# Second norm of a transformer block by halves of the tokens, and half the token subtractions on GpSimd

## The chip, the cores and the metric

The kernel runs on one core of a Trainium2 chip. The metric is device time in microseconds (us) of one execution. Five engines run their own instruction queues in order and meet only at semaphores: TensorE (PE, with its weight loads shown apart as PEld), VectorE (DVE), ScalarE (ACT), GpSimd (POOL) and SyncE (SP, which only starts DMAs).

## The reference

A block with adaptive norms (a scale, a shift and a gate for each sub-layer) over 512 tokens of width 2048. The last part of it concerns us:

```python
x = x + gt1 * merge_groups(...)             # ends in einsum('btm,md->btd', y, w_out)
h2 = rmsnorm(x, g_norm2) * (1 + sc2) + sh2
x = x + gt2 * conv_ffn(h2, rows, GRID_W, w_up, conv_w, conv_b, w_down)
```

`rmsnorm(x, g)` is `x * rsqrt(mean(x*x) + 1e-6) * g`, with the mean over the 2048 channels of a token. `conv_ffn` multiplies h2 with the gate half and the value half of `w_up`, puts the gate through a 3x3 depthwise convolution and SiLU, multiplies by the value, and projects back with `w_down`. The norm therefore stands between two dense products: no product of `w_up` can start before some token's sum over all channels is known, and that needs the last output columns of `w_out`.

## The kernel before

**Layout.** Activations lie transposed: channel on the partition, token on the free axis. The residual stream is 16 tiles `x2[k]` of 128 channels x 512 tokens. Each fp32 product is made of three products of fp32r parts: `split(hi, lo, x)` casts x to a rounded part `hi` on ACT and subtracts it on DVE (`lo`), and `mm3` accumulates hi·hi, hi·lo and lo·hi. So every weight tile costs ACT a cast (`hi_...`) and DVE a subtraction (`lo_...`) before PE can use it.

**Units.** A unit is 512 output channels as four accumulators (three for the first gate unit) in PSUM banks, over eight weight tiles kp = 0..7 of two contraction steps each. `unit_steps` loads a weight tile, splits it, and issues 6 products per accumulator and tile, each 512 tokens wide. The output projection is units `wo0` to `wo3`. The gate unit `ug0` and the value unit `uv0` follow in the same form; from `ug1` on, the units use Strassen-like sums (`seven`) with 256-wide products.

**The norm.** After each `wo` unit `residual` adds gate times accumulator to `x2[k]` on DVE, `square` squares it on ACT and adds it into a running sum `sqsq` on DVE. After `wo3` the generator `token_rstd` makes, with one-column products, the mean of each token in a 128x4 tile (`ps_rms`), takes 1/sqrt with `mean_rsqrt` (Ln and Exp on ACT, four small DVE operations as a Newton step), and spreads it over the partitions again with products against the identity (`rb_rms`). Eleven products that nothing uses (`idle_products`) stand among these. Then for each k DVE multiplies `x2[k]` with scale and rstd, ACT adds the shift and rounds (`bqh`, the high part of h2), and DVE makes the low part (`bql`). The first gate tile is read in an order that needs only the high parts first (`late`).

**Token sums.** For `seven`, the kernel makes sums and differences of token halves from h2 (`token_sums(j)`, j = 7 down to 0): per j two shifts on ACT, four 128x256 subtractions on DVE, and two splits (`bth`, `btl`). They run beside `ug0` and `uv0`. The convolution of the first gate unit (`cv`, `pads`) starts in the same stretch.

**Order.** A scheduler places the instructions on each engine by dependence and priority; `tc.high_priority()` raises what stands in it, `tc.issue_after(ins)` (wrapped by `behind(queue)`) holds an instruction back behind another, and while `pinned` is set the PE instructions keep the order of the program. Pools with few buffers set when a tile can be written: `whi` and `wlo`, the split weights of `wo`, have two buffers each.

Of the kernel before, what the change touches and what calls it, by code (L numbers as in the profile page):

```python
# [11 lines left out]
F32 = mybir.dt.float32  # L12
# [58 lines left out]
def block_kernel(ctx: ExitStack, tc: tile.TileContext, a: dict, out: bass.AP):  # L71
# [3 lines left out]
    def pool(stack, name, bufs=1, space=None, waits="pool"):  # L75
        if space is None:
            return stack.enter_context(tc.tile_pool(name=name, bufs=bufs, reuse_waits=waits))
        return stack.enter_context(tc.tile_pool(name=name, bufs=bufs, space=space, reuse_waits=waits))

    def sub(o, x, y):  # L80
        V.tensor_tensor(out=o, in0=x, in1=y, op=ALU.subtract)
# [15 lines left out]
    def mm(*args, **kw):  # L97
        ins = PE.matmul(*args, **kw)  # L98
        if pinned[0]:
            tc.keep_in_program_order(ins)  # L100
# [42 lines left out]
    def acc(name, shape=(P, T)):  # L143
        return (banks8[0] if banks8 else psA).tile(list(shape), F32, name=name, tag="acc")
# [44 lines left out]
    def load_split(src, name, n=2, w=512):  # L189
        raw = load_raw(src, name, n, w)  # L190
        with tc.high_priority():
            parts = split_new(raw, name, (n, w))
        fill()
        return parts

    def behind(queue):

        stack = ExitStack()
        for ins in queue:
            stack.enter_context(tc.issue_after(ins))  # L200
        return stack
# [10 lines left out]
            sums = split_new(s, f"b{name}", (4, HW))  # L212
        return plain, sums

    def unit_steps(src, name, xh, xl, accs, late=False, rates=None):

        n = len(accs)
        for kp in range(KP):
            if rates:
                rate[0] = rates[kp]  # L220
            wh, wl = load_split(src[kp], f"{name}_{kp}", w=P * n)
            if kp == 0 and late:

                for m, (ws, xs) in enumerate(((wh, xh), (wl, xh), (wh, xl))):
                    for k in range(2):
                        for i in range(n):
                            mm(accs[i], ws[:, k, P * i : P * i + P], xs[k], start=(m == 0 and k == 0), stop=False)
                continue
            for i in reversed(range(n)) if late and kp == KP - 1 else range(n):
                for kk in range(2):  # L230
                    k = 2 * kp + kk
                    mm3(accs[i], wh[:, kk, P * i : P * i + P], wl[:, kk, P * i : P * i + P],
                        xh[k], xl[k], k == 0, k == KT - 1)
# [783 lines left out]

    st_3 = ExitStack()
    gp = pool(st_3, "gp", 2)
    rp = pool(st_3, "rp")  # L1020
    mod_raw.append(pool(st_3, "mraw3", 4, waits="tile"))
    rate[0] = 2.2
    for g in range(4):
# [21 lines left out]
    def square(k, sums, pl, tag, sl=slice(0, T)):  # L1045

        n = sl.stop - sl.start
        first = not sums
        sq = pl.tile([P, n], F32, name=f"sq{tag}{k}", tag=f"{tag}s" if first else f"{tag}{k}" if k >= KT - 2 else tag)
        S.activation(sq, x2[k][:, sl], AF.Square)  # L1050
# [29 lines left out]
    x2d = [dram.tile([P, T], F32, name=f"x2d{k}", tag=f"x{k}") for k in range(KT)]  # L1080
    sums2 = []
    for n in range(4):
        pinned[0] = n == 3
        accs = unit(a["w_out"][n], f"wo{n}", yh, yl)
        for k in range(4 * n, 4 * n + 4):
            x2.append(ytile(k, f"x2_{k}"))
            nc.sync.dma_start(x2[k], a["xT"][k])
        with tc.high_priority():
            for i in range(4):
                residual(4 * n + i, accs[i], modc[2])  # L1090
                nc.gpsimd.dma_start(x2d[4 * n + i], x2[4 * n + i])
                square(4 * n + i, sums2, rp, "sq")
    with tc.high_priority():
        _, r2 = token_rstd(sums2, rp, "rms2", idle=4)
        idle_products(acc("idle", (P, P)), sums2[0][:, 0:P], 7)
    pinned[0] = False
    assert not fillers
    st_3.close()
    st_h.close()
# [6 lines left out]
    fp = pool(ctx, "fp", waits="tile")  # L1106
    stp = pool(ctx, "stp", 3, waits="tile")
# [4 lines left out]
    def flat(x):  # L1112
        return x.rearrange("p a b -> p (a b)")

    bq = [[operand(j, part, "q", f"bq{part}{j}", (P, 4, HW)) for j in range(KP)] for part in "hl"]
    bt = [[operand(j, part, "t", f"bt{part}{j}", (P, 3, HW)) for j in range(KP)] for part in "hl"]
    h2 = [[flat(b[k // 2][:, 2 * (k % 2) : 2 * (k % 2) + 2, :]) for k in range(KT)] for b in bq]
    with tc.high_priority():
        for k in range(KT):
            sk, bk = modc[4][:, k : k + 1], modc[3][:, k : k + 1]  # L1120
            V.scalar_tensor_tensor(out=x2[k], in0=x2[k], scalar=sk, in1=r2, op0=ALU.mult, op1=ALU.mult)
            S.activation(h2[0][k], x2[k], AF.Identity, bias=bk)
            V.scalar_tensor_tensor(out=h2[1][k], in0=x2[k], scalar=bk, in1=h2[0][k].bitcast(F32), op0=ALU.add,
                                   op1=ALU.subtract)
# [63 lines left out]

    def up_gate(q):
        if q == 0:  # L1190
            accs = unit(a["w_up3"][0], "ug0", *h2, n=3, late=True)
            with tc.high_priority():
                for i, ps in enumerate(accs):
                    S.copy(pads[:, i, 1 : ROWS + 1, 1 : GW + 1], ps.rearrange("p (r c) -> p r c", c=GW))
# [76 lines left out]
    up_gate(0)  # L1271
    st_p.close()
    banks8.append(pool(ctx, "psM", 8, PSUM, waits="tile"))
    for j in reversed(range(KP)):
        token_sums(j)
# [28 lines left out]
    halves = [slice(0, T // 2), slice(T // 2, T)]  # L1304

    class Late:
        at = {}
# [135 lines left out]
```

## Time and profile before

| | |
|---|---|
| median of 3 runs | 2513.3 us (2512.97 to 2513.51) |
| the profiled execution | 2511.87 us, span 2510.1 us |
| mean granted TensorE clock | 0.998 |
| PE busy | 2469.3 us (98%) |
| DVE busy | 1815.0 us (72%) |
| ACT busy | 1024.0 us (41%) |
| POOL busy | 182.5 us (7%) |

The span runs from the first to the last instruction, and the execution's own time is 1.8 us longer. The profiled execution is one of its own: 1.4 us under the median of the three timed ones. PE is busy nearly throughout, so what counts is where PE still waits and what is put into its queue. The norm lies at 1140 to 1149 us of the span, `ug0` follows until 1181.5 and `uv0` until 1214.

### The profile page before, as it was taken

Reading aid. Unit: us, or ns where it says so; the run is one execution under the profiler, and the core shown is the slowest. Engines: PE = TensorE matmul, PEld = TensorE weight load, DVE = VectorE, ACT = ScalarE, POOL = GpSimd, SP = SyncE. Lnnn points to the kernel's source line nnn. Section 1 sums busy time; section 2 is a strip of 40 time slices with the busy share of each in tenths; the row PEclk is TensorE's granted clock in tenths of the full one; section 3 lists DMA queues with packets and bytes.
Section 4 is the critical chain, followed back from the end, with each engine's and each line's share of the span. In section 5 each row is a group of like instructions: output and inputs, shape, how many; then the busy total and the mean of one; then the engine's idle time right before and its main releaser. Section 6 shows DMA issues by size and latency. Waiting matters only on the chain.

```text
span 2510.1 us, 39398 instructions
## 1 busy us (share of the span) xinstructions
PE 2469.3 (98%) x15740; PEld 2204.1 (88%) x15740; DVE 1815.0 (72%) x2880; ACT 1024.0 (41%) x1517; POOL 182.5 (7%) x242
## 2 busy tenths in 40 slices
PE   6999999999999999999999999999999999999998
PEld 4887889888987888888989999999999999999997
DVE  6666754554445877858988787878787878787886
ACT  4224543332213233226454444444444444444445
POOL 0000000000000000000020101010101010101022
PEclk9999999999999999999999999999999999999999
DMA  9741011123334878842373737373636363646464
GB/s 385 271 172 42 26 43 51 51 76 125 110 117 155 286 274 304 299 158 99 108 176 101 168 104 166 107 168 104 167 104 166 107 162 108 161 113 160 113 186 135
DMA packets 121552, 372.20 MB, mean 148 GB/s; under 512 B 13908, under 2 KB 18328, under 8 KB 121368
## 3 DMA queue, kind: packets, MB, share of 16 engines
q1 hardware_dynamic: 94680, 318.29, 37.7%
q0 software_dynamic: 25600, 50.34, 11.4%
q8 instruction: 123, 2.02, 0.3%
q10 hardware_dynamic: 1088, 1.05, 0.1%
q14 instruction: 61, 0.50, 0.1%
HBM read 319.30 MB, written 50.33 MB: 147 GB/s over the span
## 4 chain that ended last, share of the span: by engine, by line
PE 85%; issue 9%; DVE 2%; DMA 2%; POOL 1%; ACT 1%; SPq 0%; DVEq 0%; POOLq 0%; ACTq 0%
PE a L98 19%; PE dn L98 17%; PE uv L98 15%; PE ug L98 14%; PE ga L98 7%; PE po L98 4%; PE wo L98 3%; PE sl L98 1%; PE ps_m L98 1%; DMA raw_m<-in_w_mod 1%; PE cst L98 1%; PE s L98 1%; DMA xl<-in_xT 0%; POOL x2d L1269 0%; DMA x2d<-st 0%
## 5 line engine op out<-in xcount | busy, mean ns | idle before, releaser
L98 PE MATMUL dn<-gh,lo_d 128*128 128x512 f32 x672 | 262.3, 390 | 0.3 <-DVE lo_d L93 0.3
L98 PE MATMUL dn<-gh,hi_d 128*128 128x512 f32 x672 | 261.6, 389 | 0.0
L98 PE MATMUL dn<-gl,hi_d 128*128 128x512 f32 x672 | 261.6, 389 | 0.0
L1215 DVE SCALAR_TENSOR_TENSOR cv<-pads,cwt,cv 128x512 f32<-128x512 f32 x344 | 239.5, 748 | 0.6
L1269 POOL DMA_DIRECT2D x2d<-st x160 | 140.1, 928 | 1142.7 <-ACT st L1268 1057.5
L313 DVE SCALAR_TENSOR_TENSOR sum_m<-raw_m,csil,sum_m 128x512 f32<-128x512 f32 x240 | 180.1, 750 | 9.0 <-DMA raw_m<-in_w_mod 3.1
L93 DVE TENSOR_TENSOR lo_buv<-sum_uv,hi_buv 128x1024 fp32r<-128x1024 f32 x80 | 98.0, 1224 | 103.6 <-ACT hi_buv L92 103.6
L98 PEld LDWEIGHTS dn<-gh,lo_d 128*128 128x128 f32 x672 | 126.1, 188 | 28.9 <-DVE lo_d L93 2.6
L98 PE MATMUL a<-hi_h,hTh 128*128 128x256 f32 x512 | 150.4, 294 | 0.5 <-ACT e L406 0.5
L98 PEld LDWEIGHTS dn<-gl,hi_d 128*128 128x128 f32 x672 | 126.2, 188 | 25.9
L98 PEld LDWEIGHTS dn<-gh,hi_d 128*128 128x128 f32 x672 | 126.2, 188 | 25.6
L98 PE MATMUL a<-hi_h,hTl 128*128 128x256 f32 x512 | 144.7, 283 | 0.0
L98 PE MATMUL a<-lo_h,hTh 128*128 128x256 f32 x512 | 144.7, 283 | 0.0
L92 ACT CAST hi_d<-raw_d 128x1024 fp32r<-128x1024 f32 x86 | 88.6, 1030 | 131.9 <-PE ug L98 70.6
L93 DVE TENSOR_TENSOR lo_d<-raw_d,hi_d 128x1024 fp32r<-128x1024 f32 x86 | 102.9, 1196 | 48.1 <-ACT hi_d L92 47.5
L98 PE MATMUL ug<-bth,hi_bug 128*128 128x256 f32 x480 | 136.7, 285 | 0.1
L98 PE MATMUL uv<-bth,lo_buv 128*128 128x256 f32 x480 | 135.9, 283 | 0.8 <-DVE lo_buv L93 0.8
L98 PE MATMUL uv<-bqh,lo_auv 128*128 128x256 f32 x480 | 135.9, 283 | 0.0
L98 PE MATMUL uv<-bth,hi_buv 128*128 128x256 f32 x480 | 135.9, 283 | 0.0
L98 PE MATMUL uv<-bql,hi_auv 128*128 128x256 f32 x480 | 135.8, 283 | 0.0
L98 PE MATMUL ug<-bqh,lo_aug 128*128 128x256 f32 x480 | 135.8, 283 | 0.0
L98 PE MATMUL uv<-btl,hi_buv 128*128 128x256 f32 x480 | 135.8, 283 | 0.0
(379 smaller groups left out, 7347.2 us busy)
## 6 DMA issues: line engine op xcount, KB each, us to landing
raw_m<-in_w_mod SPq DMA_DIRECT2D x192, 512.0 KB, 5.2
raw_d<-in_w_down SPq DMA_DIRECT2D x82, 512.0 KB, 3.4
raw_ug<-in_w_up SPq DMA_DIRECT2D x80, 512.0 KB, 3.5
x2d<-st POOLq DMA_DIRECT2D x160, 256.0 KB, 5.5
raw_uv<-in_w_up SPq DMA_DIRECT2D x80, 512.0 KB, 6.2
raw_h<-in_w_heads SPq DMA_DIRECT2D x64, 512.0 KB, 3.6
raw_ga<-in_w_gates SPq DMA_DIRECT2D x32, 512.0 KB, 4.5
raw_wo<-in_w_out SPq DMA_DIRECT2D x32, 512.0 KB, 4.8
```

The lines of the kernel that those rows point to most:

```text
L92: cast[0] = S.copy(hi, x).ins
L93: return V.tensor_tensor(out=lo, in0=x, in1=hi.bitcast(F32), op=ALU.subtract).ins
L98: ins = PE.matmul(*args, **kw)
L313: V.scalar_tensor_tensor(out=parts[0], in0=x, scalar=ck, in1=parts[0], op0=ALU.mult, op1=ALU.add)
L1215: V.scalar_tensor_tensor(out=t3, in0=src, scalar=w, in1=t3, op0=ALU.mult, op1=ALU.add)
L1269: nc.gpsimd.dma_start(x2d[k], t, accum_op=ALU.add)
```

## The change

- The last unit of the output projection runs kp 0..5 as before; DVE adds these partial sums to the residual. The products of kp 6 and 7 are then made by halves of the tokens: eight groups (two halves, four accumulators) of 12 products 256 wide, each into a bank of its own, with a residual step and a square per group.
- The norm is done per half: two fp32 products of a matrix of ones against the two tiles of squares (`ss2`) give the mean already spread over the partitions, and `mean_rsqrt` works on 128x256. The one-column products, the spreading products and the eleven idle products are gone. Half 0's `ss2` stands on PE after the first group of half 1.
- h2 of k = 0..3 is made by halves, and the first two weight tiles of the gate unit, split early, are used as 72 products 256 wide: half 0 kp 0, `ss2` of half 1, half 0 kp 1, half 1 kp 0 and 1.
- The splits of gate tiles 2 and 3 are held behind half 0's low parts (`split_queue`), and later steps behind one another (`gate_queue`, `lows`, `sums_queue`).
- Two of the four subtractions of each `token_sums(j)` move to GpSimd.
- The clearing of `pads` on GpSimd and the loads of the convolution's weights come after the norm; the four stores of x2[12..15] come after half 1's residual steps.

The diff, cut to its core:

```diff
-            if kp == 0 and late:
...
-                continue
+            with behind(queue if kp < since + 2 else ()):
+                wh, wl = load_split(src[kp], f"{name}_{kp}", w=P * n)
...
+    def last_halves(steps, x, done):
+        for hf, sl in enumerate(halves):
+            for i in range(4):
+                o = acc(f"wo3_{hf}_{i}", (P, T // 2))
+                for kp, (wh, wl) in steps:
+                    for kk in range(2):
+                        k = 2 * kp + kk
+                        mm3(o, wh[:, kk, P * i : P * i + P], wl[:, kk, P * i : P * i + P],
+                            x[0][k][:, sl], x[1][k][:, sl], k == 2 * steps[0][0], k == KT - 1)
+                done(hf, i, o)
...
     with tc.high_priority():
-        _, r2 = token_rstd(sums2, rp, "rms2", idle=4)
-        idle_products(acc("idle", (P, P)), sums2[0][:, 0:P], 7)
-    pinned[0] = False
+        for i in range(4):
+            residual(12 + i, accs[i], modc[2])
+    steps = [(kp, load_split(a["w_out"][3][kp], f"wo3_{kp}")) for kp in (KP - 2, KP - 1)]
...
+    def half_norm(sl):
+        ss = psb(f"ss2_{sl.start}", (P, T // 2))
+        mm(ss, ones, sums2[0][:, sl], start=True, stop=False)
+        mm(ss, ones, last_sq[0], start=False, stop=True)
+        v, t = (rp.tile([P, T // 2], F32, name=f"{n}_{sl.start}", tag=n) for n in ("rv2", "rt2"))
+        with tc.high_priority():
+            mean_rsqrt(ss, D, v, t, r2[:, sl])
+
+    def out_done(hf, i, o):
+        k, sl = 12 + i, halves[hf]
+        with tc.high_priority():
+            residual(k, o, modc[2], sl)
+            sq = rp.tile([P, T // 2], F32, name=f"sqh{hf}_{i}", tag="sqh" if i == 3 else "sq")
+            S.activation(sq, x2[k][:, sl], AF.Square)
+            if i < 3:
+                add(sums2[0][:, sl], sums2[0][:, sl], sq)
+            else:
+                last_sq[0] = sq
+            if hf:
+                nc.gpsimd.dma_start(x2d[k], x2[k])
+        if hf and i == 0:
+            half_norm(halves[0])
...
+        for k in range(4):
+            split_queue = modulated(k, halves[0])
+    gate_queue = []
+    def gate_done(hf, kp):
+        if hf == kp == 0:
+            half_norm(halves[1])
+            with tc.high_priority():
+                for k in range(4):
+                    gate_queue[:] = modulated(k, halves[1])
+    first_halves(gsteps, ug0, h2, gate_done)
...
-        sub(half(k0, 1), half(k0, 1), half(k1, 1))
+        G.tensor_tensor(out=half(k0, 1), in0=half(k0, 1), in1=half(k1, 1), op=ALU.subtract)
         sub(half(k1, 1), half(k1, 1), half(k0, 0))
         split(flat(bt[0][j][:, 0:2, :]), flat(bt[1][j][:, 0:2, :]), x2[k0])
-        sub(rest(j), half(k1, 1), half(k1, 0))
+        G.tensor_tensor(out=rest(j), in0=half(k1, 1), in1=half(k1, 0), op=ALU.subtract)
...
-            accs = unit(a["w_up3"][0], "ug0", *h2, n=3, late=True)
+            accs = ug0
+            for _ in unit_steps(a["w_up3"][0], "ug0", *h2, accs, late=True, since=2, queue=split_queue):
+                pass
```

The first place is the norm on DVE. Before, its queue reads as follows from the last residual step on; `lo_ug0_0` is the low part of the first gate tile, `rs..._rms2` the small norm tiles, `rb_rms2` the spread rstd in PSUM.

```order
L1043 SCALAR_TENSOR_TENSOR x2_15_9433<-wo3_3_9129,mod2_62,x2_15_9433 128x512
L93 TENSOR_TENSOR lo_ug0_0_9620<-raw_ug0_0_9617,hi_ug0_0_9619 128x768
L93 TENSOR_TENSOR lo_ug0_1_9644<-raw_ug0_1_9641,hi_ug0_1_9643 128x768
L159 TENSOR_SCALAR rs1_rms2_9466<-ps_rms2_9453 128x4
L161 SCALAR_TENSOR_TENSOR rs2_rms2_9467<-rs3_rms2_9468 128x4
L84 TENSOR_TENSOR rs2_rms2_9467<-rs2_rms2_9467,rs1_rms2_9466 128x4
L163 SCALAR_TENSOR_TENSOR rs3_rms2_9468<-rs2_rms2_9467,rs3_rms2_9468 128x4
L1121 SCALAR_TENSOR_TENSOR x2_0_8405<-x2_0_8405,mod4_64,rb_rms2_9475 128x512
```

Now the norm of half 1 reads as follows, after half 0's modulation; `rv2`, `rt2` and `cst` (columns of the constants' tile that are no longer needed) are the norm's 256-wide tiles.

```order
L1183 SCALAR_TENSOR_TENSOR x2_3_8411<-x2_3_8411,mod4_64,cst_58 128x256
L1185 SCALAR_TENSOR_TENSOR bql1_9590<-x2_3_8411,mod3_63,bqh1_9582 128x256
L93 TENSOR_TENSOR lo_ug0_2_9775<-raw_ug0_2_9772,hi_ug0_2_9774 128x768
L93 TENSOR_TENSOR lo_ug0_3_9799<-raw_ug0_3_9796,hi_ug0_3_9798 128x768
L159 TENSOR_SCALAR rv2_256_9649<-ss2_256_9646 128x256
L161 SCALAR_TENSOR_TENSOR rt2_256_9650<-cst_58 128x256
L84 TENSOR_TENSOR rt2_256_9650<-rt2_256_9650,rv2_256_9649 128x256
L163 SCALAR_TENSOR_TENSOR cst_58<-rt2_256_9650,cst_58 128x256
L1183 SCALAR_TENSOR_TENSOR x2_0_8405<-x2_0_8405,mod4_64,cst_58 128x256
L1183 SCALAR_TENSOR_TENSOR x2_1_8407<-x2_1_8407,mod4_64,cst_58 128x256
```

The four small operations have become four 256-wide ones for each half, and those of half 1 stand behind the low parts of gate tiles 2 and 3, which before came only after eleven steps of the modulation.

The second place is the norm on ACT. Before, the queue there is this; `sqsq15` is the last square, `bqh` the high parts of h2, `hi_ug0_...` the high parts of gate tiles.

```order
L92 CAST hi_ug0_0_9619<-raw_ug0_0_9617 128x768
L92 CAST hi_ug0_1_9643<-raw_ug0_1_9641 128x768
L1050 ACTIVATE sqsq15_9451<-x2_15_9433 128x512
L158 ACTIVATE rs2_rms2_9467<-ps_rms2_9453,eps_66 128x4
L160 ACTIVATE rs3_rms2_9468<-rs2_rms2_9467 128x4
L1122 ACTIVATE bqh0_9528<-x2_0_8405,mod3_63 128x512
L1122 ACTIVATE bqh0_9528<-x2_1_8407,mod3_63 128x512
L1122 ACTIVATE bqh1_9529<-x2_2_8409,mod3_63 128x512
```

Now it is this, where `sqh1_...` are squares of half 1.

```order
L1148 ACTIVATE sqh1_1_9513<-x2_13_9366 128x256
L1148 ACTIVATE sqh1_2_9531<-x2_14_9368 128x256
L1184 ACTIVATE bqh0_9581<-x2_0_8405,mod3_63 128x256
L1184 ACTIVATE bqh0_9581<-x2_1_8407,mod3_63 128x256
L1148 ACTIVATE sqh1_3_9549<-x2_15_9370 128x256
L1184 ACTIVATE bqh1_9582<-x2_2_8409,mod3_63 128x256
L1184 ACTIVATE bqh1_9582<-x2_3_8411,mod3_63 128x256
L92 CAST hi_ug0_2_9774<-raw_ug0_2_9772 128x768
L92 CAST hi_ug0_3_9798<-raw_ug0_3_9796 128x768
L158 ACTIVATE rt2_256_9650<-ss2_256_9646,eps_66 128x256
L160 ACTIVATE cst_58<-rt2_256_9650 128x256
L1184 ACTIVATE bqh0_9581<-x2_0_8405,mod3_63 128x256
```

Half 1's Ln (`rt2_256`) stands behind the casts of gate tiles 2 and 3, and half 0's first `bqh` stands behind two squares of half 1.

The third place is DVE beside the first value unit, from the low part of its weight tile 5 to that of tile 6. Before, it reads as follows; `cv...` are taps of the convolution, `sum_ug1` and `lo_aug1` belong to the first Strassen-like unit, `bql4` is a low part of the token sums.

```order
L93 TENSOR_TENSOR lo_uv0_5_10023<-raw_uv0_5_10020,hi_uv0_5_10022 128x768
L87 TENSOR_TENSOR sum_ug1_0_10171<-raw_ug1_0_10169 128x512
L93 TENSOR_TENSOR lo_aug1_0_10173<-raw_ug1_0_10169,hi_aug1_0_10172 128x768
L87 TENSOR_TENSOR sum_ug1_0_10171<-sum_ug1_0_10171,raw_ug1_0_10169 128x256
L1215 SCALAR_TENSOR_TENSOR cv0_10114<-pads_9612,cwt_9608,cv0_10114 128x512
L87 TENSOR_TENSOR sum_ug1_0_10171<-sum_ug1_0_10171,raw_ug1_0_10169 128x256
L93 TENSOR_TENSOR bql4_9540<-x2_10_9102,bqh4_9532 128x256
L93 TENSOR_TENSOR lo_uv0_6_10047<-raw_uv0_6_10044,hi_uv0_6_10046 128x768
```

Now the same place reads as follows.

```order
L93 TENSOR_TENSOR lo_uv0_5_10130<-raw_uv0_5_10127,hi_uv0_5_10129 128x768
L87 TENSOR_TENSOR sum_ug1_0_10278<-raw_ug1_0_10276 128x512
L93 TENSOR_TENSOR lo_aug1_0_10280<-raw_ug1_0_10276,hi_aug1_0_10279 128x768
L87 TENSOR_TENSOR sum_ug1_0_10278<-sum_ug1_0_10278,raw_ug1_0_10276 128x256
L1308 SCALAR_TENSOR_TENSOR cv0_10221<-pads_9770,cwt_9766,cv0_10221 128x512
L87 TENSOR_TENSOR sum_ug1_0_10278<-sum_ug1_0_10278,raw_ug1_0_10276 128x256
L93 TENSOR_TENSOR bql4_9593<-x2_10_9102,bqh4_9585 128x256
L1308 SCALAR_TENSOR_TENSOR cv0_10221<-pads_9770,cwt_9766,cv0_10221 128x512
L93 TENSOR_TENSOR lo_uv0_6_10154<-raw_uv0_6_10151,hi_uv0_6_10153 128x768
```

There are two taps where one stood. From the start of the unit to `lo_uv0_6` there are now 12 taps in DVE's queue, and before there were 5; the 16 subtractions that left DVE stand on GpSimd, behind the last store of x2 and the clearing of `pads`.

More of the change, by code (lines that the diff above doesn't have):

```diff
@@ L213, in load_sums, with unit_steps @@
         return plain, sums
-    def unit_steps(src, name, xh, xl, accs, late=False, rates=None):
+    def unit_steps(src, name, xh, xl, accs, late=False, rates=None, since=0, upto=KP, queue=()):
         n = len(accs)
-        for kp in range(KP):
+        for kp in range(since, upto):
             if rates:
                 rate[0] = rates[kp]
-            wh, wl = load_split(src[kp], f"{name}_{kp}", w=P * n)
-            if kp == 0 and late:
[L224 to L227, printed above, removed]
-                continue
+            with behind(queue if kp < since + 2 else ()):
+                wh, wl = load_split(src[kp], f"{name}_{kp}", w=P * n)
             for i in reversed(range(n)) if late and kp == KP - 1 else range(n):
@@ L232, in unit_steps @@
                     mm3(accs[i], wh[:, kk, P * i : P * i + P], wl[:, kk, P * i : P * i + P],
-                        xh[k], xl[k], k == 0, k == KT - 1)
+                        xh[k], xl[k], k == 0, k == 2 * upto - 1, skip_group_check=since > 0)
                 yield 1.36
@@ L1019, in block_kernel @@
     gp = pool(st_3, "gp", 2)
-    rp = pool(st_3, "rp")
+    st_r = ExitStack()
+    rp = st_r.enter_context(tc.tile_pool(name="rp", bufs=1, side="right"))
     mod_raw.append(pool(st_3, "mraw3", 4, waits="tile"))
@@ L1080, in block_kernel @@
     x2d = [dram.tile([P, T], F32, name=f"x2d{k}", tag=f"x{k}") for k in range(KT)]
+    halves = [slice(0, T // 2), slice(T // 2, T)]
     sums2 = []
-    for n in range(4):
-        pinned[0] = n == 3
+    for n in range(3):
         accs = unit(a["w_out"][n], f"wo{n}", yh, yl)
@@ new lines, in first_halves @@
+    def first_halves(steps, accs, x, done):
+        for hf, sl in enumerate(halves):
+            for kp, (wh, wl) in steps:
+                for w, part in ((wh, 0), (wl, 0), (wh, 1)):
+                    for kk in range(2):
+                        for i, o in enumerate(accs):
+                            mm(o[:, sl], w[:, kk, P * i : P * i + P], x[part][2 * kp + kk][:, sl],
+                               start=(hf == kp == kk == part == 0 and w is wh), stop=False, skip_group_check=True)
+                done(hf, kp)
@@ new lines, in block_kernel @@
+    pinned[0] = True
+    accs = [acc(f"wo3_{i}") for i in range(4)]
+    for _ in unit_steps(a["w_out"][3], "wo3", yh, yl, accs, upto=KP - 2):
+        pass
+    for k in range(12, KT):
+        x2.append(ytile(k, f"x2_{k}"))
+        nc.sync.dma_start(x2[k], a["xT"][k])
+    with tc.high_priority():
+        for i in range(4):
+            residual(12 + i, accs[i], modc[2])
+    steps = [(kp, load_split(a["w_out"][3][kp], f"wo3_{kp}")) for kp in (KP - 2, KP - 1)]
+    gsteps = []
+    for kp in range(2):
+        raw = mod_raw[-1].tile([P, 2, 3 * P], F32, name=f"raw_ug0_{kp}", tag="raw")
+        nc.sync.dma_start(raw, a["w_up3"][0][kp])
+        parts = [rp.tile([P, 2, 3 * P], F32R, name=f"{n}_ug0_{kp}", tag=f"{n}{kp}") for n in ("gh", "gl")]
+        split(*parts, raw)
+        gsteps.append((kp, parts))
@@ new lines, in block_kernel @@
+    last_sq = [None]
+    r2 = cc(C_SEG, T)
+    def half_norm(sl):
[19 more added lines that the diff above has]
+            half_norm(halves[0])
@@ L1097, in block_kernel @@
+    last_halves(steps, (yh, yl), out_done)
     assert not fillers
@@ L1105, in block_kernel @@
     bp = pool(ctx, "bp", waits="tile")
-    fp = pool(ctx, "fp", waits="tile")
-    stp = pool(ctx, "stp", 3, waits="tile")
     def operand(j, part, what, name, shape, dtype=F32R):
@@ L1117, in block_kernel, with modulated @@
     h2 = [[flat(b[k // 2][:, 2 * (k % 2) : 2 * (k % 2) + 2, :]) for k in range(KT)] for b in bq]
-    with tc.high_priority():
[L1119 to L1124, printed above, removed]
+    def modulated(k, sl=slice(0, T)):
+        sk, bk = modc[4][:, k : k + 1], modc[3][:, k : k + 1]
+        x, hi, lo = x2[k][:, sl], h2[0][k][:, sl], h2[1][k][:, sl]
+        V.scalar_tensor_tensor(out=x, in0=x, scalar=sk, in1=r2[:, sl], op0=ALU.mult, op1=ALU.mult)
+        hi_ins = S.activation(hi, x, AF.Identity, bias=bk).ins
+        return hi_ins, V.scalar_tensor_tensor(out=lo, in0=x, scalar=bk, in1=hi.bitcast(F32), op0=ALU.add,
+                                              op1=ALU.subtract).ins
+    ug0 = [acc(f"ug0_{i}") for i in range(3)]
+    with tc.high_priority():
+        for k in range(4):
[8 more added lines that the diff above has]
+    first_halves(gsteps, ug0, h2, gate_done)
+    pinned[0] = False
+    with tc.high_priority(), behind(gate_queue):
+        lows = []
+        for k in range(4, KT):
+            with behind(lows[-2:-1]):
+                ins = modulated(k)
+                lows.append(ins[1])
+            if k == 7:
+                sums_queue = ins
+    st_r.close()
+    fp = pool(ctx, "fp", waits="tile")
+    stp = pool(ctx, "stp", 3, waits="tile")
     def half(k, i):
@@ L1190, in up_gate @@
         if q == 0:
-            accs = unit(a["w_up3"][0], "ug0", *h2, n=3, late=True)
+            accs = ug0
+            for _ in unit_steps(a["w_up3"][0], "ug0", *h2, accs, late=True, since=2, queue=split_queue):
+                pass
             with tc.high_priority():
@@ L1273, in block_kernel @@
     banks8.append(pool(ctx, "psM", 8, PSUM, waits="tile"))
-    for j in reversed(range(KP)):
-        token_sums(j)
+    with behind(sums_queue):
+        for j in reversed(range(KP)):
+            token_sums(j)
     vals = []
@@ L1303, in block_kernel @@
         nc.gpsimd.dma_start(x2[k], x2d[k])
-    halves = [slice(0, T // 2), slice(T // 2, T)]
     class Late:
```

## The prediction

> **What bounds the kernel now.** I read the page first: the engines' busy time says who can be the bound.
>
> ```profile
> PE 2469.3 (98%) x15740; PEld 2204.1 (88%) x15740; DVE 1815.0 (72%) x2880; ACT 1024.0 (41%) x1517; POOL 182.5 (7%) x242
> ```
>
> PE works 98% of the span, so a change gains only by taking time out of PE's queue or out of its few waits. Next come the windows around the norm: the last of the output projection, the norm, the gate unit in two pieces, the value unit, and a stretch of 256-wide products. The columns are length, then busy time and count of PE, PEld, DVE, ACT, POOL, then clock.
>
> ```profile
> 1100.00:1140.27 40.27, 40.27 (x192) 32.37 (x190) 10.93 (x13) 8.26 (x11) 1.08 (x2) 1.00 0.22 78
> 1140.27:1148.74 8.47, 8.22 (x55) 7.81 (x55) 4.99 (x11) 3.49 (x8) 1.09 (x2) 0.80 0.49 175
> 1157.00:1181.20 24.20, 24.20 (x108) 20.03 (x107) 24.18 (x44) 21.29 (x34) 0.00 (x0) 1.00 0.31 101
> 1181.20:1213.90 32.70, 32.70 (x146) 27.08 (x145) 32.69 (x65) 20.07 (x35) 0.00 (x0) 1.00 0.42 139
> 1220.00:1240.00 20.00, 20.00 (x169) 20.00 (x168) 20.00 (x31) 9.07 (x12) 0.00 (x0) 1.00 0.30 94
> ```
>
> Two things matter. A 512-wide product comes every 24.20 / 108 = 0.224 us and a 256-wide one every 20.00 / 169 = 0.118 us. And behind the norm PE never waits, but DVE has nothing to spare either: 24.18 of 24.20 and 32.69 of 32.70 us. What delays DVE there may delay PE. The timeline of the norm shows what PE does in its 8.47 us (start, busy, engine, line, operation).
>
> ```profile
> 1140.05 0.39 PE L98 MATMUL wo<-yTh,lo_wo 128*128 128x512 f32 x1
> 1140.64 3.10 PE L98 MATMUL ps_rms<-cst,sqsq 128*128 128x1 f32 x24 [0.21 <-DVE sqsq L87]
> 1143.79 0.27 ACT L158 ACTIVATE rs_rms<-ps_rms,eps 128x4 f32<-128x4 f32 x1 [1.26 <-PE ps_rms L98]
> 1144.08 0.20 ACT L160 ACTIVATE rs_rms<-rs_rms 128x4 f32<-128x4 f32 x1
> 1144.32 0.16 DVE L161 SCALAR_TENSOR_TENSOR rs_rms<-rs_rms 128x4 f32<-128x4 f32 x1
> 1145.46 1.69 PE L98 MATMUL rb_rms<-cst,rs_rms 128*128 128x128 f32 x8
> 1146.98 1.73 PE L98 MATMUL idle<-sqsq,cst 128*128 128x128 f32 x14
> 1147.18 2.72 DVE L1121 SCALAR_TENSOR_TENSOR x<-x,mod,rb_rms 128x512 f32<-128x512 f32 x4 [2.31 <-PE rb_rms L98]
> 1148.74 0.73 PE L98 MATMUL ug<-bqh,hi_ug 128*128 128x512 f32 x2
> ```
>
> From the start of the last product of `wo` to the first of the gate unit pass 8.69 us, where one product would take 0.22. PE counts as busy, but with small or unused products. Seven idle products show as x14: an fp32 product has two records.
>
> **The change part by part.** *Removed:* these 8.69 - 0.22 = **8.47 us**, if halves cover the norm wholly. That is the most the change can bring.
>
> *Halving:* 96 products of 256 for 48 of 512 in `wo`, 72 for 36 in the gate unit: 168 x 0.118 - 84 x 0.224 = **+1.0**. The new sums of squares are four fp32 products 256 wide; the first norm of the kernel has two of them, as four records.
>
> ```profile
> L98 PE MATMUL ss_c<-sq_c,cst 128*128 128x256 f32 x4 | 1.1, 400 | 0.0
> ```
>
> So 1.1 us per half, in PE's queue: **+2.2**. Both of these are certain.
>
> *The last weight tile of the projection.* Its split waits for a buffer that kp 5 frees.
>
> ```profile
> 1128.92 0.39 PE L98 MATMUL wo<-yTh,lo_wo 128*128 128x512 f32 x1
> 1129.12 1.05 ACT L92 CAST hi_wo<-raw_wo 128x1024 fp32r<-128x1024 f32 x1 [4.81 <-PE wo L98]
> 1129.29 0.48 PE L98 MATMUL wo<-yTh,hi_wo 128*128 128x512 f32 x1
> 1130.20 1.23 DVE L93 TENSOR_TENSOR lo_wo<-raw_wo,hi_wo 128x1024 fp32r<-128x1024 f32 x1 [0.57 <-ACT hi_wo L92]
> ```
>
> Before, kp 6 gave PE 24 x 0.224 = 5.4 us of cover from 1129.29. Now the first group needs kp 7 after six half-wide products, 0.7 us, at 1130.0; the low part, third in order, is there at 1130.20 + 1.23 = 1131.43. That is a wait of about **+1.2** (ends 0.9 and 1.4, by how much of the third product's place I count).
>
> *The first gate product.* For the chain of half 0 I need 256-wide durations.
>
> ```profile
> L158 ACT ACTIVATE scr_c<-ss_c,eps 128x256 f32<-128x256 f32 x1 | 0.5, 474 | 2.5 <-PE ss_c L98 2.5
> L160 ACT ACTIVATE rstd<-scr_c 128x256 f32<-128x256 f32 x1 | 0.4, 417 | 0.0
> L163 DVE SCALAR_TENSOR_TENSOR rstd<-scr_c,rstd 128x256 f32<-128x256 f32 x1 | 0.4, 425 | 0.0
> L1043 DVE SCALAR_TENSOR_TENSOR xf<-dl,mod,xf 128x256 f32<-128x256 f32 x8 | 3.7, 481 | 2.5 <-PE dl L98 2.5
> L1050 ACT ACTIVATE sqfq<-xf 128x256 f32<-128x256 f32 x32 | 12.1, 412 | 9.1 <-DVE xf L1043 8.2 <-DVE sqfq L87 0.8
> L93 DVE TENSOR_TENSOR lo_ug<-raw_ug,hi_ug 128x768 fp32r<-128x768 f32 x5 | 4.8, 953 | 0.0
> ```
>
> After half 0's sums: Ln 0.47, Exp 0.42, two Newton steps 0.86, a residual step of half 1 that stands between (0.48), the last Newton step 0.43, `x2_0` 0.48, another residual step 0.48, then on ACT the square behind it 0.41 and `bqh0` 0.41. That is 4.44, and eight handovers of 0.05 (Exp ended at 1144.28, DVE began at 1144.32) make 4.84. PE has three groups, 36 x 0.118 = 4.25. Stall **+0.6**.
>
> *Half 1's norm.* This is the dear place. From the first gate product PE has 36 half products and the second pair of sums, 4.25 + 1.1 = 5.35 us. DVE has in its queue ahead of the next `bqh`: an addition 0.42, three low parts 1.44, `x2_3` 0.48, the wait for its ACT step 0.41, its low part 0.48, then `lo_ug0_2` and `lo_ug0_3` 1.91, the four norm steps 1.71, `x2_0` 0.48, and ACT 0.41: 7.74, with six handovers 8.0. Half 1's first product waits **+2.7**. The ends: 0, if the scheduler's queue were met with DVE far ahead, which nothing in the sum allows, and 3.3 if every handover costs twice this.
>
> So far: -8.47 + 1.0 + 2.2 + 1.2 + 0.6 + 2.7 = **-0.8**: the stall is handed on, not removed.
>
> *The stretch behind it.* DVE loses 16 subtractions and gains 16 half steps for 8 whole ones; GpSimd gets the subtractions.
>
> ```profile
> 1179.83 1.43 DVE L81 TENSOR_TENSOR x<-x,x 128x256 f32<-128x256 f32 x4
> L1215 DVE SCALAR_TENSOR_TENSOR cv<-pads,cwt,cv 128x512 f32<-128x512 f32 x11 | 7.9, 762 | 0.0
> L1347 POOL TENSOR_TENSOR o<-xf,r3s 128x256 f32<-128x256 f32 x10 | 7.2, 748 | 35.8 <-ACT r3s L1338 35.8
> L1194 ACT COPY pads<-ug 128x512 f32<-128x512 f32 x3 | 1.8, 586 | 0.8 <-PE ug L98 0.8
> ```
>
> A subtraction costs DVE (1.43 - 0.42) / 3 = 0.34 us in a row, so 16 x 0.34 = 5.4 are saved; the half steps cost back about 1.0. But seven convolution taps more stand ahead of `lo_uv0_6` in the new order; at 0.66 each (0.76 less the overlap) that is 4.6. DVE is as full as before, and each wait of it goes through. On GpSimd a subtraction takes 0.75. DVE's third step of the last three j each follows a GpSimd step, 3 x (0.75 - 0.34) = 1.2; the casts `bth` behind GpSimd's second step pass on about as much, 1.2; and the copy of the gate's accumulators to `pads`, now behind casts that wait for GpSimd, holds the first value product for one copy, 0.6. Together **+3.0**, between 0 (all of the 5.4 as slack) and 6.5 (16 handovers of 0.41, none hidden).
>
> *Does GpSimd take DVE's time?* Two places of the trace show both at work.
>
> ```profile
> 522.43 0.29 POOL L915 TENSOR_SCALAR_AFFINE_SELECT ed<-ed 128x128 f32<-128x128 f32 x1 [59.33 <-ACT ed L912]
> 525.66 1.46 POOL L915 TENSOR_SCALAR_AFFINE_SELECT ed<-ed 128x128 f32<-128x128 f32 x3 [0.76 <-ACT ed L912]
> 525.26 1.23 DVE L93 TENSOR_TENSOR lo_h<-raw_h,hi_h 128x1024 fp32r<-128x1024 f32 x1 [0.51 <-ACT hi_h L92]
> 768.55 3.64 POOL L915 TENSOR_SCALAR_AFFINE_SELECT ed<-ed 128x128 f32<-128x128 f32 x8 [77.86 <-ACT ed L912]
> 768.15 0.69 DVE L84 TENSOR_TENSOR qs<-qs,qk 128x512 f32<-128x512 f32 x1
> 770.24 0.78 DVE L84 TENSOR_TENSOR qs<-qs,qk 128x512 f32<-128x512 f32 x1
> ```
>
> A GpSimd step of 0.29 alone became three in 1.46 while DVE read two tiles, and DVE's 0.69 became 0.78 beside GpSimd. So they do exclude each other, at least 0.09 per step for a small GpSimd step. For a step of 0.75 the price lies between 0.09 and 0.75; most of the steps here stand on a full DVE, so I take a third of the upper end, 0.25: 16 x 0.25 = **+4.0** (ends 1.4 and 12.0).
>
> The Trainium skill ("SBUF — State Buffer", section "SBUF: two separate sides") says that a DVE operation with two SBUF inputs and a GpSimd operation that reads SBUF hold a shared port pair as an exclusive lock for the whole instruction. The rows above agree as far as they go. By that rule alone, with DVE always the one that waits, the term would be the upper end, 12.0.
>
> The sum: -0.8 + 3.0 + 4.0 = **+6.2**, so 2511.9 + 6.2 = 2518.1 for an execution like the profiled one. The median of the runs stands 1.4 above that one, so I forecast **2519.5**. Differences of under 0.2% (5.0 us) I count as the same, about what a measurement of this kernel can tell from no change: 2508.3 to 2518.3.
>
> **The rivals.** *No contention:* GpSimd and DVE share without loss beyond 0.09 per step, and the last term shrinks to at most 1.4. For it: the second of the two places. Against: the first. -0.8 + 3.0 + 0.7 = +2.9, 2516.2, within 0.2%.
>
> *Everything is covered* (not slower): the low parts of gate tiles 2 and 3 and the norm of half 1 run early enough, and the 5.4 us that DVE saves absorb every wait for GpSimd. What remains is -8.47 + 1.0 + 2.2 + 1.2 = -4.1, 2509.2; without the wait for `lo_wo` -5.3, 2508.0. It decides at the first product of half 1: if DVE's 8.0 us are 5.4, it holds. Against it is the sum of rows above.
>
> *Full lock:* each GpSimd subtraction holds DVE for its 0.75. Waits for GpSimd's results then lie inside that time, so 12.0 takes the place of 4.0 and of the 2.4 of waits: -0.8 + 0.6 + 12.0 = +11.8, 2525.1. For it: the place at 525 us. Against: a DVE step that started first makes GpSimd wait instead.
>
> A smaller one: the clock. In the norm's window the granted clock was 0.80, and PE then lost nothing that counted. After a wait of 2.7 us full-size products could run slower for a while; 8.47 x 0.20 = 1.7 us is what that window lost. It lies inside my range.
>
> **How the numbers follow.** Forecast (+4 to +9) 0.45; no contention 0.25; everything covered 0.15, of which 0.04 below 2508.3; full lock 0.15. Faster is 0.04. The same is the rest of "covered" (0.11), no contention (0.25) and the lowest part of the forecast (0.04): 0.40. Slower 0.56. The range goes from 2509.2 (covered) to 2525.1 (full lock), leaving out about half of each of these two, 0.15. The forecast's own range is 2517 to 2522.5.
>
> **What would show it.** In the new profile: a PE wait of about 1.2 at `lo_wo` of the first half group; a wait under 1 at the first gate product and of 2 to 3 at half 1's, ended by ACT's `bqh`; PE waits for `lo_uv` in the value unit; DVE operations of 256 columns beside GpSimd longer than 0.42. I am wrong if the first product of half 1 follows its predecessor closely, or if the value unit still takes 32.7 us.

## The result

The changed kernel takes 2524.27 us (median of 6 runs, 2520.43 to 2525.23) and the kernel before 2513.14 in the runs beside it: a ratio of 1.0041 with a 95% interval of 1.0028 to 1.0054, or 10.3 us slower (7.0 to 13.6). The profiled execution has a span of 2520.1 us, against 2510.1. The page shows what has grown:

```profile
PE 2470.4 (98%) x15778; PEld 2206.0 (88%) x15778; DVE 1825.0 (72%) x2888; ACT 1027.0 (41%) x1527; POOL 200.5 (8%) x258
```

PE works as long as before, to 1.1 us. DVE, which was to be relieved, works 10 us longer, and POOL 18. So 8.9 of the 10 us are idle time of PE. The timeline of PE has these places (start, busy, operation, in brackets the idle time and what ended it); the rows without a bracket are landmarks, the first product of gate tile 2 and of the first Strassen-like unit.

```profile
1132.44 0.39 PE L98 MATMUL wo<-yTh,lo_wo 128*128 128x256 f32 x1 [0.76 <-DVE lo_wo L93]
1144.58 1.02 PE L98 MATMUL ug<-bqh,gh_ug 128*128 128x256 f32 x6 [0.46 <-ACT bqh L1184]
1152.60 1.02 PE L98 MATMUL ug<-bqh,gh_ug 128*128 128x256 f32 x6 [2.64 <-ACT bqh L1184]
1156.99 0.88 PE L98 MATMUL ug<-bqh,hi_ug 128*128 128x512 f32 x3
1184.23 0.50 PE L98 MATMUL uv<-bqh,hi_uv 128*128 128x512 f32 x1 [1.94 <-ACT pads L1287]
1194.79 0.50 PE L98 MATMUL uv<-bqh,hi_uv 128*128 128x512 f32 x1 [2.06 <-ACT hi_uv L92]
1197.24 0.79 PE L98 MATMUL uv<-bqh,lo_uv 128*128 128x512 f32 x1 [1.72 <-DVE lo_uv L93]
1224.08 0.28 PE L98 MATMUL ug<-bqh,hi_aug 128*128 128x256 f32 x1
```

The landmarks of the kernel before, and where kp 6 of the last `wo` unit begins in the changed one:

```profile
1157.04 0.39 PE L98 MATMUL ug<-bqh,hi_ug 128*128 128x512 f32 x1
1181.52 0.39 PE L98 MATMUL uv<-bqh,hi_uv 128*128 128x512 f32 x1
1214.15 0.28 PE L98 MATMUL ug<-bqh,hi_aug 128*128 128x256 f32 x1
```

```profile
1130.25 0.36 PE L98 MATMUL wo<-yTh,hi_wo 128*128 128x256 f32 x1
```

Counted from kp 6 of the last `wo` unit (1129.29 before, 1130.25 now):

| until the first product of | before | now | difference |
|---|---|---|---|
| gate tile 2 | 27.75 | 26.74 | -1.0 |
| the value unit | 52.23 | 53.98 | +1.75 |
| the Strassen-like unit | 84.86 | 93.83 | +9.0 |

(The remaining 1 us of the span lies ahead of kp 6, where nothing was changed; the first `wo` product differs by as much between the two executions, and by some 2 us between others.) So between these two executions the part up to gate tile 2 is 1.0 us shorter (the clock has a share in that, as e8 shows below), and the stretch behind it, where GpSimd subtracts, costs 10. In the value unit the granted clock falls too, at the second of the two waits and behind it (columns as in the prediction, the clock is the number after POOL):

```profile
1195.00:1200.00 5.00, 3.28 (x9) 2.26 (x9) 5.00 (x9) 2.19 (x6) 2.25 (x2) 0.62 0.24 79
1200.00:1205.00 5.00, 5.00 (x17) 4.00 (x16) 4.93 (x9) 2.79 (x5) 0.00 (x0) 0.70 0.26 82
1205.00:1210.00 5.00, 5.00 (x23) 4.14 (x23) 5.00 (x8) 1.35 (x3) 0.00 (x0) 1.00 0.32 105
```

A product counts as busy for 0.39 us but the next may follow after 0.22, so a wait costs 0.17 more than its idle time. The value unit grew from 32.63 to 39.85 us: 2.23 + 1.89 for the two waits, and the other 3.1 fits the clock, of which the first two rows lack 5 x 0.38 + 5 x 0.30 = 3.4 us, a part of it while PE stood. The groups of DVE and POOL in this stretch show why DVE was late:

```profile
L1185 DVE SCALAR_TENSOR_TENSOR bql<-x,mod,bqh 128x512 fp32r<-128x512 f32 x12 | 9.6, 824 | 0.1
L1183 DVE SCALAR_TENSOR_TENSOR x<-x,mod,cst 128x512 f32<-128x512 f32 x12 | 9.1, 784 | 0.0
L93 DVE TENSOR_TENSOR btl<-x,bth 128x512 fp32r<-128x512 f32 x8 | 6.4, 812 | 0.0
L81 DVE TENSOR_TENSOR x<-x,x 128x256 f32<-128x256 f32 x8 | 5.7, 747 | 2.0 <-POOL x L1230 2.0
L93 DVE TENSOR_TENSOR btl<-x,bth 128x256 fp32r<-128x256 f32 x8 | 4.8, 614 | 0.0
L1233 POOL TENSOR_TENSOR x<-x 128x256 f32<-128x256 f32 x8 | 9.2, 1166 | 6.7 <-DVE btl L93 6.7
L1230 POOL TENSOR_TENSOR x<-x,x 128x256 f32<-128x256 f32 x8 | 8.3, 1046 | 15.0 <-ACT x L1228 12.7 <-DVE x L81 2.4
```

Before, the same five groups took 747, 743, 692, 422 and 425 ns. A 256-wide subtraction of DVE takes 0.75 or 0.61 on average in place of 0.42, and one of GpSimd 1.05 to 1.17 in place of 0.75: each engine holds up the other.

Two of the three new waits are ended by ACT, behind casts that waited for GpSimd or for a late DVE. The clearest is the value unit's wait for `hi_uv`; ACT's rows ahead of it are these:

```profile
1192.10 0.62 ACT L92 CAST bth<-x 128x512 fp32r<-128x512 f32 x1 [2.92 <-POOL x L1230]
1193.91 0.83 ACT L92 CAST hi_uv<-raw_uv 128x768 fp32r<-128x768 f32 x1
```

The cast of `hi_uv` stands behind a cast of the token sums that waited 2.92 us for a subtraction of GpSimd.

### The profile page after: what moved, and what is told of

The parts are those of the page before. It is cut to its first block, busy times and chain, and to the rows that moved or that the text cites. A ratio compares the mean times of both kernels' runs of the same rounds, so it can differ in the third digit from the quotient of the medians.

```text
span 2520.1 us, 39519 instructions
## 1 busy us (share of the span) xinstructions
PE 2470.4 (98%) x15778; PEld 2206.0 (88%) x15778; DVE 1825.0 (72%) x2888; ACT 1027.0 (41%) x1527; POOL 200.5 (8%) x258
## 3 DMA queue, kind: packets, MB, share of 16 engines
q10 hardware_dynamic: 1088, 1.05, 0.1%
## 4 chain that ended last, share of the span: by engine, by line
PE 46%; issue 3%; DVE 2%; DMA 1%; POOL 0%; ACT 0%; DVEq 0%; POOLq 0%; ACTq 0%
PE uv L98 16%; PE dn L98 15%; PE ug L98 14%; DMA raw_uv<-in_w_up 1%; DVE cv L1308 1%; DVE lo_d L93 0%; DMA x2d<-st 0%; PE dl L98 0%; DVE btl L93 0%; DVE o L84 0%; POOL x L1233 0%; ACT hi_d L92 0%; POOL x L1230 0%; PE ps_rmsf L98 0%; DVE o L1437 0%
## 5 line engine op out<-in xcount | busy, mean ns | idle before, releaser
L307 DVE SCALAR_TENSOR_TENSOR sum_m<-raw_m,csil,sum_m 128x512 f32<-128x512 f32 x240 | 180.0, 750 | 10.3 <-DMA raw_m<-in_w_mod 4.3
L98 PE MATMUL ug<-bqh,hi_aug 128*128 128x256 f32 x480 | 135.8, 283 | 0.0
```

The lines of the kernel that those rows point to most:

```text
L307: V.scalar_tensor_tensor(out=parts[0], in0=x, scalar=ck, in1=parts[0], op0=ALU.mult, op1=ALU.add)
```

## The experiments

The theory: GpSimd's subtractions cost the 10 us, mainly because GpSimd and DVE shut each other out of SBUF while DVE is full. Rivals: the reordering around them costs it; only the waits for GpSimd's results cost it; the clock costs it.

**e1, the subtractions back on DVE.**

```diff
-        G.tensor_tensor(out=half(k0, 1), in0=half(k0, 1), in1=half(k1, 1), op=ALU.subtract)
+        sub(half(k0, 1), half(k0, 1), half(k1, 1))
...
-        G.tensor_tensor(out=rest(j), in0=half(k1, 1), in1=half(k1, 0), op=ALU.subtract)
+        sub(rest(j), half(k1, 1), half(k1, 0))
```

> The changed kernel with all 32 token subtractions back on DVE; the norm by halves stays. If GpSimd is what costs the 9.8 us behind the first six gate products, what is left is the norm's own balance of -0.8 us: 1 to 2 us faster than before or the same, no PE wait over 1 us in the value unit, granted clock 1.00 there. Rival: the reordering (splits held back, pads later) costs it: then it stays 6 us or more slower than before, with the waits on pads and on hi_uv still there. The 2.6 us wait of half 1's first gate product should stay in both.

Measured: 1.0001 (0.9992 to 1.0010) of before. The table of PE's waits from 1120 to 1270 us (total, times, longest) has only those of the norm left, and the clock falls behind the long one:

```profile
PE ug L98 <- ACT bqh L1184: 3.1, 2, 2.6
PE wo L98 <- DVE lo_wo L93: 0.8, 1, 0.8
```

```profile
1152.00:1156.00 4.00, 4.00 (x23) 4.00 (x23) 3.36 (x7) 1.72 (x5) 0.00 (x0) 0.59 0.20 67
```

The reordering that stays in e1 is not the cause. (The taps go back with the subtractions: 4 stand ahead of `lo_uv0_6` here, against 12 in the changed kernel.) The norm's 1.0 us is missing here; the clock's lower share takes 4 x 0.41 = 1.6 us. In the changed kernel's own profile it did not fall behind the same wait.

**e2, only the subtractions on GpSimd**, in the kernel before (the diff of e1 turned round).

> The kernel before, with its norm as it was, and only the 16 token subtractions on GpSimd. If GpSimd is the cost, 5 to 10 us slower than before, with PE waits in the value unit for lo_uv or hi_uv that before did not have. Rival (the reordering costs, not GpSimd): within 1 us of before, since DVE gets 5.4 us of work less.

Measured: 1.0028 (1.0016 to 1.0039), 7 us slower. PE's waits:

```profile
PE uv L98 <- DVE lo_uv L93: 3.5, 2, 1.9
PE uv L98 <- ACT hi_uv L92: 2.0, 2, 1.4
```

The kernel before gets new waits for `lo_uv` and `hi_uv` from GpSimd alone (not the one for `pads`), although DVE is handed 5.4 us less work by the prediction's estimate.

**e3, dummy subtractions that nobody waits for.**

```diff
         split(bt[0][j][:, 2, :], bt[1][j][:, 2, :], half(k1, 1))
+        for c in range(2):
+            G.tensor_tensor(out=scr, in0=bt[1][j][:, c, :].bitcast(F32), in1=bt[1][j][:, 2, :].bitcast(F32),
+                            op=ALU.subtract)
```

> The kernel before with 16 extra GpSimd subtractions of the same size beside it, whose result nothing reads (two for each j, behind its last low part); the rest is untouched, the output is that of before. Nobody waits for GpSimd, so only the sharing of SBUF is left. If GpSimd and DVE shut each other out, DVE's 256-wide subtractions beside them take 0.8 to 1.0 us in place of 0.42 and the kernel is 2 to 7 us slower. Rival (only the waits for GpSimd's results cost): DVE's durations stay, and the time is within 0.5 us of before.

Measured: 1.0027 (1.0017 to 1.0038). DVE's order is that of before, row for row. Its timeline has pairs of equal steps, the first of each before 1200 us, the second after it, when GpSimd's steps get through beside them. Below them stand GpSimd's own rows:

```profile
1198.77 0.94 DVE L93 TENSOR_TENSOR lo_uv<-raw_uv,hi_uv 128x768 fp32r<-128x768 f32 x1
1199.63 0.41 DVE L93 TENSOR_TENSOR bql<-x,bqh 128x256 fp32r<-128x256 f32 x1
1203.43 0.97 DVE L93 TENSOR_TENSOR bql<-x,bqh 128x256 fp32r<-128x256 f32 x1
1205.47 1.49 DVE L93 TENSOR_TENSOR lo_uv<-raw_uv,hi_uv 128x768 fp32r<-128x768 f32 x1
```

```profile
1177.28 2.01 POOL L1145 TENSOR_TENSOR scr<-btl 128x256 f32<-128x256 f32 x2 [34.64 <-DVE btl L93]
1180.05 2.22 POOL L1145 TENSOR_TENSOR scr<-btl 128x256 f32<-128x256 f32 x2 [0.76 <-DVE btl L93]
1185.32 27.74 POOL L1145 TENSOR_TENSOR scr<-btl 128x256 f32<-128x256 f32 x12 [3.04 <-DVE btl L93]
```

A GpSimd step that gets through costs a DVE step about half a us whatever its size (0.41 to 0.97, 0.94 to 1.49). Step by step against the trace of before, sixteen DVE steps are longer, as many as there are dummies, by 0.46 to 0.55 us each and 8.2 in all. That alone, with no result waited for, accounts for a loss as large as e2's. The row of 27.74 us shows the other side: the first of its twelve steps lasts 15.34 us, from 1185.32 to 1200.66, and until 1200 DVE's steps all have their normal length.

**e4, useless products against the clock**, in the changed kernel.

```diff
+    idle = acc("idle", (P, HW))
+    pinned[0] = True
-    for _ in unit_steps(a["w_up3"][1], "uv0", *h2, accs):
-        pass
+    for n, _ in enumerate(unit_steps(a["w_up3"][1], "uv0", *h2, accs)):
+        if n == 5:
+            for _ in range(4):
+                mm(idle, ones, cc(C_ID, HW), start=True, stop=True)
+    pinned[0] = False
```

> The changed kernel with four products of constants (fp32, 256 wide, about 2.3 us of PE, result unused) put into PE's queue at the place where it waits 2.1 us for hi_uv in the value unit. If the lower granted clock behind the waits (0.62 and 0.70) costs 3.4 us, useless work makes the kernel 1 to 3 us faster than the changed kernel, 2521 to 2523 us, with a clock near 1.00 there. Rival (the clock follows something else, or costs nothing): the same as the changed kernel or up to 1 us slower.

Measured: 1.0037 (1.0025 to 1.0050), no different from the changed kernel: the gain of 1 to 3 us did not come. PE's waits:

```profile
PE uv L98 <- DVE lo_uv L93: 3.8, 3, 1.8
PE uv L98 <- ACT pads L1287: 1.9, 1, 1.9
PE uv L98 <- ACT hi_uv L92: 0.4, 1, 0.4
```

In the value unit the clock stayed at 1.00, and a new wait of 1.8 us for `lo_uv` came later. DVE looks like the bound there, and slow products filled time in which PE would have waited. The scheduler also put three taps more ahead of that `lo_uv`, so how much of the 3.1 us was free time is not settled.

**e5, useless products in half 1's wait**, on e1. PE is pinned there, so the other engines' order is that of e1.

```diff
                 done(hf, kp)
+            if hf == 0:
+                for _ in range(4):
+                    mm(idle, ones, cc(C_ID, T // 2), start=True, stop=True)
```

> As e1 (halves, all subtractions on DVE), with four products of constants (fp32, 256 wide, result unused) in PE's queue where it waits 2.6 us for the first product of half 1. The order on the other engines is that of e1. In e1's trace the clock fell to 0.59 behind this wait, which cost about 1.5 us. If that is why the halves bring nothing, the wait shrinks to under 1 us, the clock stays at 1.00, and the kernel is 1 to 1.5 us faster than e1, about 1 us faster than before. Rival (the clock falls in any case, or its time was hidden): the same as e1.

Measured: 0.9991 (0.9982 to 1.0000), an interval that still overlaps e1's. The clock stays at 1.00, and the wait is filled (x8 are the four products):

```profile
1148.87 1.89 PE L98 MATMUL idle<-cst 128*128 128x256 f32 x8
1151.67 1.02 PE L98 MATMUL ug<-bqh,gh_ug 128*128 128x256 f32 x6 [0.92 <-ACT bqh L1187]
```

**e6, two accumulators at a time**, on e1.

```diff
-            for i in range(4):
-                o = acc(f"wo3_{hf}_{i}", (P, T // 2))
+            for pair in ((0, 1), (2, 3)) if hf == 0 else ((0,), (1,), (2,), (3,)):
+                outs = {i: acc(f"wo3_{hf}_{i}", (P, T // 2)) for i in pair}
                 for kp, (wh, wl) in steps:
+                    for i in pair:
```

> As e1, but in half 0 the last two weight tiles of the output projection are used for two accumulators at a time (kp 6 for both, then kp 7 for both), so that kp 7 is wanted 0.7 us later. If the 0.76 us wait for lo_wo is paid in full, the kernel is 0.6 to 0.7 us faster than e1 and the wait is under 0.2. Rival: later waits take it back (the first gate product then waits 0.5 us more), no gain.

Measured: 0.9997 (0.9988 to 1.0006). The wait falls by 0.5, not to under 0.2, and the later ones keep their length:

```profile
1131.94 0.39 PE L98 MATMUL wo<-yTh,lo_wo 128*128 128x256 f32 x1 [0.28 <-DVE lo_wo L93]
```

Half a us is less than these runs can tell from e1.

**e7, both of these.**

> Both of the two: halves with all subtractions on DVE, pairs in half 0, and the four products of constants in the wait of half 1. If both gains hold, 1 to 2 us faster than before (2511 to 2514 where before is 2513 to 2515), the fastest of all. If the norm's balance is only what the waits leave, within 1 us of before.

Measured: 0.9989 (0.9981 to 0.9998): 2.8 us faster than before, the first version that is clear of it.

**e8, GpSimd writing only**, in the kernel before; a tiny copy on ACT makes the writes start where e3's dummies did.

```diff
         split(bt[0][j][:, 2, :], bt[1][j][:, 2, :], half(k1, 1))
+        S.copy(scr[:, 0:4], bt[1][j][:, 2, 0:4].bitcast(F32))
+        for c in range(4):
+            G.memset(scr, float(c))
```

> The kernel before with 32 GpSimd memsets of 128x384 (about 0.42 us each, 13 us in all) started at the same places as the dummy subtractions of e3 by a tiny ACT copy; GpSimd then writes to SBUF but reads nothing. If only a GpSimd operation that reads SBUF shuts out DVE, DVE's durations stay at 0.42 and the time is within 1 us of before. If any GpSimd operation does, DVE's steps beside it grow and the kernel is 3 to 7 us slower, as e3 was.

Measured: 0.9998 (0.9989 to 1.0007). GpSimd is busy for 13.4 us at the same places, and DVE does not feel it:

```profile
L1146 POOL MEMSET scr<- 128x384 f32 x32 | 13.4, 419 | 41.6 <-ACT scr L1144 40.2
L81 DVE TENSOR_TENSOR x<-x 128x256 f32<-128x256 f32 x16 | 6.5, 419 | 0.0
L93 DVE TENSOR_TENSOR btl<-x,bth 128x256 fp32r<-128x256 f32 x8 | 3.4, 420 | 0.0
```

So GpSimd steps that only write, here a memset, do not hold DVE up, and those of e3, which read, do. The Trainium skill ("SBUF — State Buffer", section "SBUF: two separate sides") has the exclusive lock for a DVE operation with two SBUF inputs only against a GpSimd operation that reads SBUF; e3 and e8 agree.

This execution also shows what the norm of before takes when the clock holds. The granted clock was 1.00 from 1140 to 1160 us, and from the last product of `wo` to the first of the gate unit it is 7.51 us, not 8.69:

```profile
1142.33 0.39 PE L98 MATMUL wo<-yTh,lo_wo 128*128 128x512 f32 x1
1149.84 1.67 PE L98 MATMUL ug<-bqh,hi_ug 128*128 128x512 f32 x6
```

**e9, the splits of gate tiles 2 and 3 later**, on e7 with two useless products.

```diff
+                    if k == 1:
+                        late_queue[:] = gate_queue
...
-            for _ in unit_steps(a["w_up3"][0], "ug0", *h2, accs, late=True, since=2, queue=split_queue):
+            for _ in unit_steps(a["w_up3"][0], "ug0", *h2, accs, late=True, since=2, queue=late_queue):
```

> As e7, but the splits of gate tiles 2 and 3 are held behind half 1's second low part in place of half 0's, so that they no longer stand ahead of half 1's norm, and two products of constants in place of four. If those two splits make half 1 late, its wait with the constants' 1 us counted in falls from 2.6 to about 1.5 us, and 0.5 to 1 us is gained on e7; the splits then make gate tile 2 late by up to 0.8, so the net may be as small as 0.3. Rival: it all returns as a wait at gate tile 2, no gain on e7 or a loss of up to 0.5.

Measured: 0.9990 (0.9981 to 0.9998), no different from e7. The wait moved, as the rival had it:

```profile
1149.58 1.02 PE L98 MATMUL ug<-bqh,gh_ug 128*128 128x256 f32 x6 [0.49 <-ACT bqh L1189]
1154.96 0.96 PE L98 MATMUL ug<-bqh,hi_ug 128*128 128x512 f32 x3 [0.67 <-ACT bqh L1189]
```

**e10, eight dummies in place of sixteen**: as e3, with `range(1)`.

> As e3, with one dummy GpSimd subtraction for each j (8 in place of 16). If each holds DVE for 0.53 us, as its stretched steps in e3 show, DVE loses 4.2 us in place of 8.5; with about 0.8 to 1 us of slack ahead of PE the kernel is 2.5 to 4 us slower than before. Rival (a fixed loss, such as a clock drop once DVE is late at all): about as slow as e3, 6 us.

Measured: 1.0018 (1.0008 to 1.0027), 4.5 us slower: between the two expectations, nearer to the first. One wait is left, and one GpSimd step stands for long:

```profile
PE uv L98 <- DVE lo_uv L93: 2.8, 1, 2.8
```

```profile
1185.68 20.81 POOL L1145 TENSOR_TENSOR scr<-btl 128x256 f32<-128x256 f32 x6 [3.38 <-DVE btl L93]
```

The clock fell behind the wait:

```profile
1205.00:1210.00 5.00, 2.64 (x9) 2.15 (x10) 5.00 (x7) 0.52 (x1) 1.42 (x2) 0.86 0.29 89
1210.00:1215.00 5.00, 5.00 (x19) 4.01 (x18) 4.44 (x9) 1.88 (x3) 0.00 (x0) 0.79 0.72 223
```

DVE's loss goes with the number of GpSimd steps: in this trace eight steps of DVE are longer, by 4.0 us in all, against sixteen and 8.2 in e3. The whole time does not settle it: the intervals of e3 and e10 overlap, and e10's covers half of e3's loss.

## Why the prediction was right, and where it was not

The forecast was slower, 2519.5 with a range up to 2525.1; 2524.27 lies inside, near the upper end, and above the 2517 to 2522.5 that the prediction gave for its own mechanism. By its own steps, each wait with 0.17 added:

- *Norm and halving, up to gate tile 2*: forecast -0.8, measured -1.0. The wait for `lo_wo` was 0.9 (forecast 1.2), the first gate product's 0.6 (0.6), half 1's 2.8 (2.7). The queue order and the durations of before gave these waits to a few tenths. That the sum fits as well is in part luck. The 8.47 us to be removed held 1.2 of lower clock, which the prediction called a loss of nothing that counted; e8 shows 7.51 in place of 8.69. From kp 6 to gate tile 2 it is 26.60 us in e8, with the old norm at a full clock, and 26.74 here, with halves at a full clock. Where the clock fell, it is 27.75 before, 27.82 in e3 and 29.10 in e10, and with halves 28.21 in e1 and 28.25 in e4. Like with like, the norm by halves as it stands brings nothing, as e1's 1.0001 says too.
- *The wait for the copy to `pads`*: forecast 0.6, measured 2.1. The accumulators' copy stands behind two casts of the token sums, one of which waited 0.53 us for GpSimd and one 0.74 for a subtraction of DVE. GpSimd's steps took 1.05 to 1.17, not 0.75, and DVE's were longer too; this term was mis-sized by that.
- *The taps*: of the 4.6 us that the prediction charged for seven taps more ahead of `lo_uv0_6`, nothing shows as a wait. The last wait of the value unit ends at 1197.24, and the first tap starts at 1199.79. In e4, where the clock held, a later `lo_uv` with nine taps ahead of it did come 1.8 us late, so the slow clock may have covered them. (The terms of this stretch add up to 3.2, not 3.0: 1.0 + 4.6 - 5.4 is left out.)
- *GpSimd taking DVE's time*: this term was too small. I took 0.25 per step as a third of the upper end; e3 shows 0.46 to 0.55. In the changed kernel the stretched steps of DVE sum to 6.5 us (the five groups shown above, each count by its growth; 2.6 of it on `x<-x,x` alone), and 2.0 of waits for GpSimd come on top; the 5.4 saved do not cover them. How PE's loss divides between stretched steps and waits for GpSimd's results is not separated by a run: e3 prices the first alone, and in the changed kernel both stand in the same chains.
- *The clock*: left out of the sum as a small matter inside the range. The value unit lost about 3.1 us to it. Without it the whole would be close to the forecast, though by luck, since the terms missed in both directions (the taps too dear, the copy and GpSimd too cheap); and e4 suggests that part of that time would have come back as waits for DVE.
- *The rivals*: "no contention" is refuted by e3, "full lock" (+11.8) is nearest in size, but for a partly different reason, half a us per step, waits for results and the clock. "Everything is covered" failed at half 1's first product, as the sum said.

What stays open: why the clock fell behind half 1's wait of 2.64 us in e1 and e4, and not behind the same wait in the changed kernel and in e6.

## What to carry to other kernels

Work moved from a full DVE to GpSimd need not be relief. Here DVE's steps had two SBUF inputs and GpSimd's read SBUF, and a 0.42 us step saved could cost DVE 0.46 to 0.55, while the moved step waited as well; GpSimd steps that only wrote cost nothing. Where a norm is overlapped by halves, look for what the scheduler puts ahead of the second half's chain: the stall moves there. And where a wait of 2 to 3 us ahead of dense products cannot be removed, products of constants in PE's queue can keep the clock up: it held in all three profiles with them (e5, e7, e9), and in two of four without. They help only where PE and not another engine is late. A gain of 1 us between two profiles can be the clock alone: compare executions in which it fell with others in which it fell.

## What was not expected

- A GpSimd step that is shut out can stand for long: in e3 for 15.34 us and in e10 for 15.33, while DVE's steps followed one another without a gap, nearly all at their normal length. From 1200 us on, with DVE as full, GpSimd's steps got through one after another; what let them in is open.
- A DVE step beside a GpSimd step grew by 0.46 to 0.55 us, not by the 0.75 that a GpSimd step takes alone and that the rival "full lock" charges.
- The granted clock fell to 0.59 behind a single wait of 2.64 us in e1, and to 0.78 and 0.79 over the 8 us around the end of the same wait in e4. The Trainium skill ("TensorE: Matmul & The Clock Gate", section "HAM oscillation — how this bites in real kernels") sets the bound at idle gaps of over about 3.4 us; here a shorter one was enough in two executions and not in two others.
